# A four-layer diffusion backbone on one core: two activation tiles moved by 32 bytes in memory

## The chip, the cores and the metric

The kernel runs on one core of a Trainium2 chip. The metric is the time of one execution on the device in microseconds; the median of a few executions is compared. Profiles come from one profiled execution each.

## The reference

One inference step of a backbone with four layers, on 128 context tokens and 512 latent tokens of width 1024. Each layer is a token mixer and a squared-ReLU MLP, each with modulation, a gate, a scaled residual and a layer norm behind it:

```python
for l in range(DEPTH):                      # DEPTH = 4
    kind, j = l % N_MIXERS, l // N_MIXERS   # 0 linear attention, 1 conformer, 2 short convolution
    mp, ms = adaln(c_ctx, ...), adaln(c, ...)
    op, os_ = mixer(modulate(xp, mp[0], mp[1])), mixer(modulate(xs, ms[0], ms[1]))
    xp = layer_norm(ALPHA * xp + mp[2] * op, ln_g[l, 0], ln_b[l, 0])
    xs = layer_norm(ALPHA * xs + ms[2] * os_, ln_g[l, 0], ln_b[l, 0])
    fp = sqrelu_mlp(modulate(xp, mp[3], mp[4]), ff_w1[l], ff_w2[l])
    fs = sqrelu_mlp(modulate(xs, ms[3], ms[4]), ff_w1[l], ff_w2[l])
    xp = layer_norm(ALPHA * xp + mp[5] * fp, ln_g[l, 1], ln_b[l, 1])
    xs = layer_norm(ALPHA * xs + ms[5] * fs, ln_g[l, 1], ln_b[l, 1])

def sqrelu_mlp(h, w1, w2):                  # 1024 -> 4096 -> 1024
    return jnp.square(jax.nn.relu(h @ w1)) @ w2

def short_conv(h, w_in, w_conv, w_out, grid):
    bg, cg, u = jnp.split(h @ w_in, 3, axis=-1)
    u = dw_conv(cg * u, w_conv, GRID_W if grid else 1)
    return (bg * u) @ w_out
```

Layers 0 and 3 have linear attention, layer 1 the conformer convolution, layer 2 the short convolution.

## The kernel before

All 640 tokens (five token tiles of 128; tile 0 is the context) stay on the chip: x0 to x4 hold them token by token, and hT holds the next sublayer's input feature by feature, in eight k tiles of 128 features. Weights stream from memory in tiles of 128x1024 float32. To keep float32 accuracy with the faster number type float32r, every operand of a large product is split in two parts, hi and lo, and a product is three: hi·hi, hi·lo and lo·hi. For weights `split` (L104 to L109) does that: ScalarE copies hi into tile whi, VectorE subtracts and gives wlo. For activations the same is done in `put_hT` (L394 to L399) into hT, in the MLP's `evac` (L1156 to L1164) into tile act, and in the short convolution's `evac` (L1100 to L1125) into the tiles a0 to a7, called a in the profile.

There are two kinds of products, and TensorE's order is written by hand:

- mm1 (L138 to L172, product at L143): the weight tile is stationary, hT moves past it in a piece of 384 tokens and one of 256. One output bank takes 8 k tiles x 3 = 24 products.
- mm2 (L175 to L195, product at L189): the activations are stationary, 512 columns of a weight tile move past them. Again 24 products fill an output bank, one bank for each token tile; five banks are a pass over one half of the output's 1024 columns. The stationary operand is act in the MLP, a in the short convolution and hT in linear attention and the conformer. Banks are called mm and mx in the profile, by the pool that they come from.

```python
for h, a in ((0, 0), (0, 1), (1, 0)):
    self.nc.tensor.matmul(
        ps, lhs(kt, h, t), s[a][:, c + cols.start:c + cols.stop], start=(i == 0), stop=(i == 3 * nk - 1)
    )
```

The MLP (L1144 to L1180) goes over four blocks of 1024 hidden features. In each, mm1 makes eight act tiles, and mm2 runs two passes of 120 products with them. So a layer's MLP has eight passes, and in the very last one of the kernel the last token tile is done in two halves of 256 columns (`finish`, L900). The short convolution (L1086 to L1133) runs two passes with a, in `out_proj`.

Between these products stand others: transposes for the layer norm (L408), which `ln` puts 6.2 us behind a tile's statistics by a clock of the program's own, which counts a product of n columns as n / 2400 us (`beat`, L93); and, in the MLPs before layers 1 to 3, the modulation of the next layer. VectorE adds up that modulation's products in tile acc (L316 to L320), and TensorE sums acc over its partitions (L338) and transposes the result (L298).

Tiles of a sublayer come from a pool that is opened for it and gets the memory behind the permanent pools, in the order in which the tiles are declared. In the program before the change the tiles begin at these bytes of each partition: hT at 17696; the weight tiles at 104480 and every 4096 from there to 149536; acc at 178176; the two buffers of r at 182272 and 184832; the eight buffers of act at 187392 and every 5120 from there; in the short convolution cu0 at 178176, cu1 at 181280, a0 to a7 at 184384 and every 5120 from there, y at 225344. Divided by 64, hT and the weight tiles leave a rest of 32; acc, r, act, cu0, a and y leave 0. hT's parts for a k tile and a token tile lie at multiples of 512 bytes from its beginning, and so do those of act and a.

The conformer's pool begins at the same place, with u0 (4096 bytes) and u1 (4096 bytes), which GpSimd fills with zeros in this order.

Of the kernel before, what the change touches and what calls it, by code (L numbers as in the profile page):

```python
# [7 lines left out]
F32 = mybir.dt.float32  # L8
# [30 lines left out]
class Filler:  # L39
    """Products for the tensor engine to run while a chain of dependent steps waits for other engines."""  # L40

# [25 lines left out]
class Net:  # L67
# [19 lines left out]

# [1 line left out]
    def after(self, us, fn):  # L89
# [12 lines left out]

# [1 line left out]
    def split(self, src, n=1024):  # L104
# [14 lines left out]
    @contextmanager  # L119
    def behind(self, t):  # L120
        """Keeps the vector engine's work in it behind the parts of token tile t's next input."""
        with ExitStack() as held:
            for half in range(2 if (t, 0) in self.marks else 0):
                held.enter_context(self.tc.issue_after(self.marks[t, half]))
            yield
# [10 lines left out]

# [1 line left out]
    def mm1_steps(self, ps, w, c0, n, m=128):  # L138
        """Yields the microseconds of each instruction, as the other generators of products do."""
        i = 0  # L140
        for kt in range(KT):
            for a, h in ((0, 0), (0, 1), (1, 0)):
                self.nc.tensor.matmul(  # L143
                    ps[:m, :n], w[a][:, kt * m:(kt + 1) * m], self.hT[:, h, kt, c0:c0 + n],
                    start=(i == 0), stop=(i == 3 * KT - 1),
                )
                i += 1
                yield self.beat(n / 2400)
# [24 lines left out]

# [1 line left out]
    def mm2(self, srcs, lhs, epi):  # L175
# [31 lines left out]

# [1 line left out]
    def mod_queue(self, l):  # L209
        """Queues layer l's modulation by groups of 2048 columns: a k tile at a time on the tensor engine, or,  # L210
        where the groups fall in an MLP, two k tiles of 512 columns at a time on the vector engine."""
        self.mods[l] = {"T": self.modp.tile([128, 48, 2], F32, tag="modT", name="modT", bufs=3)}
        for g in range(1 if l == self.layers[0] else 0, 3):
            if (l, g) in MOD_DVE:
                for v in (2 * g, 2 * g + 1):
                    for half in range(2):
                        for p in range(4):
                            self.fill.append((l, g, partial(self.mod_dve, l, v, half, p)))
            else:
                for kt in range(KT):  # L220
                    self.fill.append((l, g, partial(self.mod_step, l, g, kt)))
# [21 lines left out]
    def tail(self, us, fn):  # L243
        """Runs fn once: us later, or before the next part of a modulation."""
        def once():
            if self.mod_tail is once:
                self.mod_tail = None
                fn()

        self.mod_tail = once  # L250
        self.after(us, once)

    def mod_bank(self, l, cols):
        """A bank for the sums, and the bias of each quarter of its rows."""
        ps = self.ps.tile([128, 512], F32, tag="md", name="md", bufs=1)
        mrow = self.row.tile([128, 512], F32, tag="mrow", name="mrow")
        n = 128 // len(cols)
        for t, c in enumerate(cols):
            self.nc.gpsimd.dma_start(
                mrow[n * t:n * t + n, :], self.d["mod_b"][l:l + 1, c:c + 512].broadcast_to([n, 512]))  # L260
        return ps, mrow
# [39 lines left out]
    def mod_dve(self, l, v, half, p):  # L301
        """Vector v's half: two k tiles more of the products, added up per partition; the tensor engine sums those."""
        nc, m = self.nc, self.mods[l]
# [44 lines left out]
    def affine(self, l, sub, prev):  # L348
        """A, B with modulate(LN(x)) = xhat * A + B per feature; prev = (l, i) of the LN."""
        nc = self.nc  # L350
# [23 lines left out]

# [1 line left out]
    def stats(self, a, b, eps):  # L376
        """mean, (var + eps) ** -0.5 and -mean * that over two [128, 512] halves."""
        nc = self.nc
        st = self.small.tile([128, 2, 6], F32, tag="bn", name="bn")
        nc.vector.bn_stats(st[:, 0], a)  # L380
        nc.vector.bn_stats(st[:, 1], b)
        mv = self.moments(st, eps)
        nc.gpsimd.tensor_scalar(out=mv[:, 4:5], in0=mv[:, 0:1], scalar1=mv[:, 3:4], scalar2=-1.0, op0=AL.mult, op1=AL.mult)
        return mv
# [9 lines left out]
    def put_hT(self, hf, k0, t):  # L394
        """hf [128, n, 128]: features of k tiles k0.. of token tile t, split into hT."""
        dst = lambda h: self.hT[:, h, k0:k0 + hf.shape[1], t * 128:(t + 1) * 128]
# [50 lines left out]

# [1 line left out]
    def start(self):  # L449
# [27 lines left out]
    def opening(self, products, raw, tmp):  # L477
        """The first sublayer's input, k tile by k tile as its shift and scale come in: unit u of the first
        layer's modulation holds those of features 128 u.. for all inputs. products(u): what tile u is for."""
        nc = self.nc  # L480
        parts = {}
# [56 lines left out]

# [1 line left out]
    def gla(self, l, j, nxt):  # L540
        nc, d, tc = self.nc, self.d, self.tc
        with ExitStack() as ctx:
# [8 lines left out]
            def gate_w(dst, hd):  # L551
                """Two heads of the gates' second factor, against z_hi, z_lo, z_hi and 1, 1: w_hi, w_hi, w_lo, b_hi, b_lo."""
                st = self.stage.tile([128, 1024], F32, tag="st", name="st")
# [112 lines left out]
            def chunks(a, par):  # L666
                """[128, 640] -> the chunks of one parity: [128, 5, 64]."""
                return a.rearrange("p (c b k) -> p c b k", b=2, k=64)[:, :, par]
# [4 lines left out]
            def core1(hd):  # L673
# [34 lines left out]
                for i in range(2):  # L708
# [3 lines left out]
                    self.mark = nc.vector.tensor_tensor(out=Em[i], in0=q[hd, 1], in1=Em[i], op=AL.mult)  # L712
                # per tile: the keys of the chunk that comes first, decayed to its end, and both chunks' decay
                F1 = q[hd, 0].rearrange("p (d c k) -> p d c k", d=2, k=64)
# [171 lines left out]
    def out_proj(self, w, lhs, nxt, last):  # L886
        """The sublayer's last product with the residual, and the layer norm token tile by token tile."""
        self.mm2(w[0], lhs, self.residual(0))
        self.out_last(w, lhs, nxt, last)
# [10 lines left out]
    def finish(self, w, lhs):  # L900
        """The last token tile, its second half of columns in two parts to have less to do after the last product."""
        nc, t = self.nc, TT - 1
# [31 lines left out]

# [1 line left out]
    def conformer(self, l, j, nxt):  # L936
        nc, d, tc = self.nc, self.d, self.tc
        with ExitStack() as ctx:
# [50 lines left out]
            def convolve(c, scr, meanwhile=None):  # L989
                """Four taps of 32 channels a pass: partition (s, channel) holds the row shifted by s."""  # L990
                f = 5 * ROW
# [21 lines left out]
            def add_bias():  # L1013
                """x += b_pw2 * gate, for the second product's bias."""
                self.flush()
# [68 lines left out]

# [1 line left out]
    def shortconv(self, l, j, nxt):  # L1086
        nc, d, tc = self.nc, self.d, self.tc
        with ExitStack() as ctx:
            sb = ctx.enter_context(tc.tile_pool(name="sc", bufs=1))
            cus = []  # L1090
            for i in range(2):
                cu = sb.tile([128, 770], F32, name=f"cu{i}")
                nc.gpsimd.memset(cu, 0.0)
                cus.append(cu)
# [47 lines left out]

# [1 line left out]
    def mlp(self, l, ln_next, last):  # L1144
        nc, d, tc = self.nc, self.d, self.tc
        with ExitStack() as ctx:
            sb = ctx.enter_context(tc.tile_pool(name="mlp", bufs=1))
            self.acc = sb.tile([128, 2, 512], F32, name="acc")
            self.load_gate(l, "g2")
# [37 lines left out]
    def more_banks(self, more):  # L1187
        """Three banks more for products, except where linear attention has them."""
        if not more:
# [23 lines left out]
def _layout(inp):  # L1213
# [3 lines left out]
    A = {}  # L1217
# [22 lines left out]
    def stat(w, order=None):  # L1240
        """[1024, M] -> output tiles [M/128, 128, 8 * 128]."""
        t = w.reshape(KT, 128, -1, 128).transpose(2, 1, 0, 3)
        return (t if order is None else t[order]).reshape(-1, 128, KT * 128)

    def mov(w):
        """[1024, 512 n] -> [n, 4, 128, 2 * 512]."""
        return w.reshape(4, 2, 128, -1, 512).transpose(3, 0, 2, 1, 4).reshape(-1, 4, 128, 1024)
# [51 lines left out]
```

## Time and profile before

| | |
|---|---|
| median of 3 runs | 3054.25 us |
| lowest and highest | 3054.06 and 3059.77 us |
| profiled execution, first to last instruction (span) | 3051.8 us |
| TensorE (PE) busy | 3003.6 us, 98%, 17452 products |
| its weight loads (PEld) | 2619.4 us, 86% |
| VectorE (DVE) busy | 1850.7 us, 61% |
| ScalarE (ACT) busy | 998.5 us, 33% |
| GpSimd (POOL) busy | 153.6 us, 5% |
| memory traffic, mean | 115 GB/s |
| mean granted clock of TensorE | 0.996 of full speed |

How to read it: "busy" is the time in which an engine had at least one instruction under way. Products overlap, so a product's own duration (its start to its end) is longer than the interval from its start to the next one's. A line such as L189 is the line of the kernel that issued the instruction; `mx<-whi,act` names the tile written and the tiles read. The profile does not say which of the tiles read is stationary; the code does.

### The profile page before, as it was taken

The numbers are of one execution on the slowest core, as the hardware profiler recorded it, in microseconds if no ns is written. First come the engines' busy times: TensorE is split into PE (matmuls) and PEld (weight loads), VectorE is DVE, ScalarE is ACT, GpSimd is POOL, SyncE is SP. The second block draws the span as 40 slices with busy tenths as digits, with TensorE's granted clock in tenths as the row PEclk, the third lists the DMA queues.
The fourth block names the chain that finished last, engine by engine and source line by source line (L and its number), as shares of the span: only waits on it lengthen the run. The fifth ranks groups of instructions, "written<-read, shape, count | busy, mean of one in ns | idle before, by whom it ended". The sixth has DMA issues, their size and how long they took to land.

```text
span 3051.8 us, 42170 instructions
## 1 busy us (share of the span) xinstructions
PE 3003.6 (98%) x17452; PEld 2619.4 (86%) x17452; DVE 1850.7 (61%) x2737; ACT 998.5 (33%) x1592; POOL 153.6 (5%) x295
## 2 busy tenths in 40 slices
PE   7999999999999899999999999999999999999998
PEld 5887798898898697888999988988988887998997
DVE  4445877767597775775384485773465448644345
ACT  4333433232242351332242152321344434322221
POOL 0000100000010010000010010000010001000000
PEclk9999999999999999999999999999999999999999
DMA  6334244445164425453232133552213312222120
GB/s 245 120 121 162 87 132 155 152 144 171 62 182 127 129 97 163 148 174 97 72 111 77 63 118 107 170 162 66 82 69 120 104 64 89 101 90 74 58 90 35
DMA packets 101792, 350.28 MB, mean 115 GB/s; under 512 B 12940, under 2 KB 18572, under 8 KB 101600
## 3 DMA queue, kind: packets, MB, share of 16 engines
q1 hardware_dynamic: 91888, 317.79, 31.6%
q0 software_dynamic: 9712, 29.80, 3.0%
q8 instruction: 137, 2.24, 0.3%
q14 instruction: 55, 0.45, 0.0%
HBM read 340.29 MB, written 7.24 MB: 114 GB/s over the span
## 4 chain that ended last, share of the span: by engine, by line
PE 95%; DVE 2%; DMA 1%; ACT 1%; issue 1%; POOL 0%; SPq 0%; DVEq 0%; POOLq 0%; ACTq 0%
PE mx L143 23%; PE mm L189 22%; PE mx L189 21%; PE mm L143 18%; PE md L273 1%; PE mx L1003 1%; PE md L338 1%; PE tp L408 1%; PE tp L777 1%; PE o L797 1%; PE o L763 1%; PE tp L747 1%; PE tp L724 1%; PE mm L1003 0%; ACT whi L107 0%
## 5 line engine op out<-in xcount | busy, mean ns | idle before, releaser
L107 ACT CAST whi<-st 128x1024 fp32r<-128x1024 f32 (+1 forms) x378 | 395.7, 1050 | 1118.1 <-PE mx L189 301.4
L143 PE MATMUL mx<-hT,whi 128*128 128x256 f32 (+1 forms) x3216 | 706.8, 310 | 1.6 <-DVE hT L398 1.3
L108 DVE TENSOR_TENSOR wlo<-st,whi 128x1024 fp32r<-128x1024 f32 (+1 forms) x378 | 460.0, 1221 | 377.7 <-ACT whi L107 375.9
L143 PE MATMUL mm<-hT,whi 128*128 128x384 f32 (+1 forms) x2592 | 566.6, 309 | 1.2 <-DVE hT L398 0.7
L143 PEld LDWEIGHTS mx<-hT,whi 128*128 128x128 f32 x3216 | 541.9, 189 | 6.0 <-DVE hT L398 2.8
L143 PE MATMUL mx<-hT,wlo 128*128 128x384 f32 (+1 forms) x1608 | 497.8, 310 | 0.0
L189 PE MATMUL mx<-whi,act 128*128 128x512 f32 (+1 forms) x1536 | 493.6, 395 | 0.0
L143 PEld LDWEIGHTS mm<-hT,whi 128*128 128x128 f32 x2592 | 434.1, 189 | 5.4 <-DVE hT L398 1.6
L143 PE MATMUL mm<-hT,wlo 128*128 128x256 f32 (+1 forms) x1296 | 399.7, 308 | 0.0
L189 PEld LDWEIGHTS mx<-whi,act 128*128 128x128 f32 x1536 | 287.4, 187 | 70.8 <-issue 1.7
L189 PE MATMUL mm<-whi,act 128*128 128x512 f32 (+1 forms) x1040 | 336.2, 394 | 0.0
L143 PEld LDWEIGHTS mx<-hT,wlo 128*128 128x128 f32 x1608 | 304.4, 189 | 2.5 <-issue 2.5
L189 PE MATMUL mx<-wlo,act 128*128 128x512 f32 (+1 forms) x768 | 303.4, 395 | 0.0
L320 DVE SCALAR_TENSOR_TENSOR acc<-st,cm,acc 128x512 f32<-128x512 f32 x392 | 275.8, 745 | 36.0 <-ACT acc L318 34.6
L189 PE MATMUL mm<-whi,hT 128*128 128x512 f32 x888 | 286.1, 395 | 0.0
L143 PEld LDWEIGHTS mm<-hT,wlo 128*128 128x128 f32 x1296 | 245.3, 189 | 7.2 <-issue 6.7
L189 PEld LDWEIGHTS mm<-whi,act 128*128 128x128 f32 x1040 | 194.5, 187 | 47.8 <-issue 1.7
L189 PE MATMUL mm<-wlo,act 128*128 128x512 f32 (+1 forms) x520 | 205.1, 394 | 0.0
L189 PEld LDWEIGHTS mm<-whi,hT 128*128 128x128 f32 x888 | 165.5, 188 | 31.9
L204 DVE TENSOR_TENSOR mx<-mx,gate 128x512 f32<-128x512 f32 x120 | 83.5, 696 | 172.7 <-PE mx L189 172.6
L189 PEld LDWEIGHTS mx<-wlo,act 128*128 128x128 f32 x768 | 144.0, 187 | 41.0 <-issue 7.5
L189 PE MATMUL mm<-wlo,hT 128*128 128x512 f32 x444 | 177.3, 399 | 0.0
(250 smaller groups left out, 3157.8 us busy)
## 6 DMA issues: line engine op xcount, KB each, us to landing
st<-in_w SPq DMA_DIRECT2D x256, 512.0 KB, 3.6
st<-in_modv SPq DMA_DIRECT2D x112, 512.0 KB, 4.1
st<-in_modw SPq DMA_DIRECT2D x80, 512.0 KB, 4.7
st<-in_gvr SPq DMA_DIRECT2D x32, 512.0 KB, 5.5
st<-in_cpw SPq DMA_DIRECT2D x24, 512.0 KB, 4.9
st<-in_scin SPq DMA_DIRECT2D x24, 512.0 KB, 3.5
ur<-uscr SPq DMA_DIRECT2D x40, 238.0 KB, 5.9
st<-in_gqk SPq DMA_DIRECT2D x16, 512.0 KB, 5.1
```

The lines of the kernel that those rows point to most:

```text
L107: self.nc.scalar.copy(hi[:, :n], src)
L108: self.nc.vector.tensor_tensor(out=lo[:, :n], in0=src, in1=hi[:, :n].bitcast(F32), op=AL.subtract)
L143: self.nc.tensor.matmul(ps[:m, :n], w[a][:, kt * m:(kt + 1) * m], self.hT[:, h, kt, c0:c0 + n], start=(i == 0), stop=(i == 3 * KT - 1),)
L189: self.nc.tensor.matmul(ps, lhs(kt, h, t), s[a][:, c + cols.start:c + cols.stop], start=(i == 0), stop=(i == 3 * nk - 1))
L204: self.nc.vector.tensor_tensor(out=ps, in0=ps, in1=g, op=AL.mult)
L273: nc.tensor.matmul(ps[32 * t:32 * t + 32, :], self.cm[:, kt, :], st[t // 2][:, c:c + 512], start=(kt == 0), stop=(kt == KT - 1),)
L320: nc.vector.scalar_tensor_tensor(out=acc[:, s], in0=w, scalar=c, in1=acc[:, s], op0=AL.mult, op1=AL.add)
L338: nc.tensor.matmul(ps[r:r + 32, :], self.ones, acc[:, s], start=True, stop=True)
L408: nc.tensor.transpose(tp[:, i * 128:(i + 1) * 128], x[:, k * 128:(k + 1) * 128], self.ident)
L724: nc.tensor.matmul(sp[:, i, dd], self.tri[:, 2 + dd], G[:, t0 + i, dd], start=True, stop=True)
L747: nc.tensor.matmul(sc[:, i], Em[i][:, ts], Ep[i][:, ts], start=True, stop=True)
L763: nc.tensor.matmul(o[t], P[t % 2][:, 2], v[t], start=(t % 2 == 0), stop=False)
```

## The change

Tile acc of the MLP gets 8 more columns of float32 (32 bytes) and is used through a view of the old shape. Everything declared behind it in that pool, r and act, begins 32 bytes later. In the short convolution cu0 gets 8 more columns, so cu1, a and y begin 32 bytes later: act at 187424, a0 at 184416. The work is otherwise the same. The rest of the diff takes out comments and docstrings and changes no instruction.

```diff
 # shortconv
             for i in range(2):
-                cu = sb.tile([128, 770], F32, name=f"cu{i}")
+                cu = sb.tile([128, 770 + 8 * (1 - i)], F32, name=f"cu{i}")
                 nc.gpsimd.memset(cu, 0.0)
                 cus.append(cu)
 # mlp
             sb = ctx.enter_context(tc.tile_pool(name="mlp", bufs=1))
-            self.acc = sb.tile([128, 2, 512], F32, name="acc")
+            self.acc = sb.tile([128, 1032], F32, name="acc")[:, :1024].rearrange("p (s c) -> p s c", s=2)
```

## Rows read from the trace of the kernel before

**Rows 1.** The page: span, TensorE's busy time, the chain that ended last by engine.

```profile
span 3051.8 us, 42170 instructions
...
PE 3003.6 (98%) x17452; PEld 2619.4 (86%) x17452; DVE 1850.7 (61%) x2737; ACT 998.5 (33%) x1592; POOL 153.6 (5%) x295
...
PE 95%; DVE 2%; DMA 1%; ACT 1%; issue 1%; POOL 0%; SPq 0%; DVEq 0%; POOLq 0%; ACTq 0%
```

**Rows 2.** TensorE's waits: who waited for whom, us in total, times, longest.

```profile
PE mx L189 <- DVE x L205: 2.5, 2, 1.3
...
PE mx L143 <- DVE hT L398: 1.3, 4, 0.5
```

**Rows 3.** Groups of L189, TensorE: shape, count | busy us, mean ns | idle before.

```profile
L189 PE MATMUL mx<-whi,act 128*128 128x512 f32 x1520 | 490.8, 396 | 0.0
...
L189 PE MATMUL mm<-whi,act 128*128 128x512 f32 x1024 | 333.3, 395 | 0.0
...
L189 PE MATMUL mx<-wlo,act 128*128 128x512 f32 x760 | 301.2, 396 | 0.0
L189 PE MATMUL mm<-whi,hT 128*128 128x512 f32 x888 | 286.1, 395 | 0.0
...
L189 PE MATMUL mm<-wlo,act 128*128 128x512 f32 x512 | 202.9, 396 | 0.0
```

**Rows 4.** Timeline of TensorE, first products of banks: start us, us, what.

```profile
597.34 0.39 PE L189 MATMUL mm<-whi,act 128*128 128x512 f32 x1
...
608.54 0.39 PE L189 MATMUL mm<-whi,act 128*128 128x512 f32 x1
...
1055.76 0.39 PE L189 MATMUL mx<-whi,hT 128*128 128x512 f32 x1
...
1066.64 0.39 PE L189 MATMUL mx<-whi,hT 128*128 128x512 f32 x1
...
1738.65 0.40 PE L189 MATMUL mm<-whi,a 128*128 128x512 f32 x1
...
1749.85 0.40 PE L189 MATMUL mm<-whi,a 128*128 128x512 f32 x1
```

**Rows 5.** Windows: us, busy PE, PEld, DVE, ACT, POOL (count), clock, DMA share, GB/s.

```profile
585.00:614.00 29.00, 29.00 (x125) 22.43 (x124) 22.19 (x31) 4.49 (x5) 3.01 (x6) 1.00 0.55 174
...
1733.00:1762.00 29.00, 29.00 (x127) 23.36 (x127) 14.18 (x18) 5.54 (x6) 0.00 (x0) 1.00 0.10 35
```

**Rows 6.** Timeline of TensorE behind eight transposes in the conformer, every third product.

```profile
1074.55 0.39 PE L189 MATMUL mx<-wlo,hT 128*128 128x512 f32 x1
...
1075.24 0.39 PE L189 MATMUL mx<-wlo,hT 128*128 128x512 f32 x1
...
1075.94 0.39 PE L189 MATMUL mx<-wlo,hT 128*128 128x512 f32 x1
...
1076.62 0.39 PE L189 MATMUL mx<-wlo,hT 128*128 128x512 f32 x1
```

**Rows 7.** Timeline in shortconv: a tile's normalisation on ScalarE, its transposes on TensorE.

```profile
1777.27 0.82 ACT L426 ACTIVATE x<-x,mv 128x512 f32<-128x512 f32 x1 [0.30 <-POOL mv L383]
...
1780.12 1.04 PE L408 MATMUL tp<-ident,x 128*128 128x128 f32 x8
```

**Rows 8.** Timeline of TensorE, products of 256 columns: mm1, then the last token tile.

```profile
628.19 0.28 PE L143 MATMUL mx<-hT,wlo 128*128 128x256 f32 x1
...
629.27 0.28 PE L143 MATMUL mx<-hT,wlo 128*128 128x256 f32 x1
...
3036.30 0.28 PE L189 MATMUL mx<-wlo,act 128*128 128x256 f32 x1
...
3038.78 0.28 PE L189 MATMUL mx<-wlo,act 128*128 128x256 f32 x1
```

**Rows 9.** Groups of VectorE: writes of 640 columns to act and to hT.

```profile
L1163 DVE TENSOR_TENSOR act<-r,act 128x640 fp32r<-128x640 f32 x128 | 105.4, 823 | 67.3 <-ACT act L1162 67.2
...
L531 DVE TENSOR_TENSOR hT<-h,hT 128x640 fp32r<-128x640 f32 x8 | 6.5, 818 | 0.9 <-ACT hT L530 0.8
```

## The prediction

> **What bounds the kernel now.** I read the page's busy shares first: TensorE is busy in 98% of the 3051.8 us span, and the chain that ended last lies on it for 95% [rows 1]. So the time is the number of products times the interval from one start to the next. Next the list of TensorE's waits: the only entry on a product of L189, where act and a are used, is 2.5 us behind x [rows 2], and the list of groups shows that the 128x512 products of act had no idle time before them [rows 3]. A faster feed would cure nothing there; the interval is what is left to look at.
>
> The mean duration of a product does not show it. 128x512 products take 395 or 396 ns with act stationary and 395 ns with hT [rows 3], because they overlap. The timeline does show it. One output bank takes 24 products, and the bank's name changes between mm and mx, so the first products of banks can be subtracted. With act stationary, two banks go from 597.34 to 608.54: 11.20 us for 48 products, **233.3 ns** each. With a stationary, 1738.65 to 1749.85: again 11.20 us, **233.3 ns**. With hT stationary, 1055.76 to 1066.64: 10.88 us, **226.7 ns** [rows 4]. The moving operand is of one kind in all three (a 512-column half of a weight tile), as are width, number type and count. The stationary tile differs.
>
> Is it traffic on the chip? The table of windows says no [rows 5]. Both stretches have a granted clock of 1.00 (the 2.4 GHz level); around act VectorE is busy for 22.2 of 29 us at a DMA share of 0.55, around a for 14.2 of 29 us at 0.10, and the interval is the same. What act and a share, and hT does not, is their place by 64 bytes: rest 0, against 32 for hT and for the weight tiles that stream past them.
>
> **The change part by part.**
>
> *Products of act and a.* With act there are 1520 + 1024 + 760 + 512 = 3816 products of 512 columns [rows 3], with a 2 passes of 5 token tiles of 24, which is 240: together 4056. After the change both tiles have the rest of hT. If that sets the interval, each product starts 6.67 ns sooner: 4056 x 6.67 ns = **27.0 us** off TensorE, which is the path.
>
> [...]
>
> *Finding the short interval again after a break.* Behind eight transposes (L408) three products of hT take 0.69 us (1074.55 to 1075.24), the next three 0.70 us (to 1075.94), and then 0.68 again (to 1076.62) [rows 6]. That is 0.03 us lost per break, which act at its present interval need not lose. The lower count of breaks is the 17 starts behind mm1 (16 blocks of the four MLPs and the short convolution; the second pass of each follows the first directly), 17 x 0.03 = 0.5 us. The upper count adds every group of transposes of the layer norms (7 sublayers x 5 tiles x 2 = 70) and every group of modulation sums (14 vectors x 2 halves = 28): 115 x 0.03 = 3.5 us. Many of those fall between products of mm1 or of hT, so I take half, 58 breaks: **1.7 us** given back.
>
> *Layer norm behind the last product.* The code puts a tile's transposes 6.2 us of its own clock behind its statistics, and that clock counts 213 ns a product. TensorE now gets there 0.2 us sooner (6.2 / 0.213 = 29 products x 6.67 ns). In shortconv the transposes of a tile start at 1780.12, and the normalisation that they read ends at 1777.27 + 0.82 = 1778.09 [rows 7]: 2 us of slack hide 0.2. The first products of the next mm1 do wait for the split of hT, 1.3 us in four waits [rows 2], and that chain starts at the last products. The lower end is 0. The upper end gives back all that is saved in the last pass of the four sublayers that use act or a and are followed by another: 4 x 120 x 6.67 ns = 3.2 us. The existing waits are short, nearest to the lower end: **0.3 us** given back.
>
> *The last token tile.* Its second half of columns runs as 48 products of 256 columns. With act these take 118.1 ns (3036.30 to 3038.78, 2.48 us for 21). Products of this width in mm1, both of whose operands have rest 32, take 120.0 ns (628.19 to 629.27, 1.08 us for 9) [rows 8]. So equal rests are 1.9 ns slower at this width: 48 x 1.9 ns = 0.1 us, left out of the sum.
>
> *The other engines on the moved tiles.* r, act, cu1, a and y move along. VectorE subtracts 128x640 in 823 ns to act (rest 0) and in 818 ns to hT (rest 32) [rows 9]: nothing to see beyond 5 ns, and ScalarE's copies, of which I show no row, are bounded alike. act and a are written 136 times, each by a copy and a subtraction, all beside products; were that cover gone, 136 x 2 x 5 ns = 1.4 us either way. The memset of cu0 has 8 more elements on GpSimd. All of this costs nothing on the path.
>
> *Waits between pools.* A shift by 32 bytes could make a tile overlap one more old tile. By the sizes the one new overlap is at the conformer's start, u1 with the end of acc, and u0 already waits for acc, ahead of it on the same queue. No DMA moves past another. Nothing is added.
>
> *Sum:* -27.0 + 1.7 + 0.3 = -25.0 us. The profiled span of 3051.8 us becomes 3026.8. The median of the runs, 3054.25 us, is 2.45 us above the span, which is what lies around it, and becomes **3029.3 us**.
>
> **The rivals.**
>
> *No effect, since the interval goes by something else (0.11).* act and a lie in the upper part of the memory and hT in the lower, and their steps between k tiles differ (5120 and 2560 bytes). A rule by region or by step would explain the three intervals as well, and the change touches neither: 3054 us. The same time would come if the shift were rounded away, but the addresses are multiples of 32, so 32 bytes do move a tile. Against it: in mm1 the weights, from a third region, are stationary, and 120.0 ns [rows 8] exceeds 256 columns at 2.4 GHz (106.7) by 13.3 ns, just as hT's 226.7 exceeds 213.3. Only act and a exceed it by 20.0. [...]
>
> *Slower, since equal rests settle at a worse interval (0.04).* At 256 columns this is seen: 120.0 against 118.1 ns. If act at 512 columns did the same, which decides itself at 233.3 ns, the price would be 4056 x 1.9 ns = 7.7 us: 3062 us. Against it stands hT at 512 columns.
>
> *Half the gain, since breaks come too often (0.05).* If act stayed in the unsettled 0.69 to 0.70 us for three [rows 6] in half of its products, about 13.5 us would be gained: 3040.7 us. Against it: hT settles within six to eight products, and a bank has 24.
>
> **How the numbers follow.** The forecast has 0.80. Its own bounds are gains of 27.0 - 0.5 + 1.4 = 27.9 and 27.0 - 3.5 - 3.2 - 1.4 = 18.9 us, 3026.4 to 3035.4. The runs shown spread to 5.5 us above the median, so I reach to 3042, which also takes in the half gain, and to 3024 below. No effect and slower stay outside. A measurement of this kernel can tell about 0.2% (6.1 us) from no change; within that lies the second case alone: faster 0.85, same 0.11, slower 0.04.
>
> **What would show it.** Right: two banks of act or a in 10.88 us in place of 11.20; the counts of products and the intervals of hT and mm1 as before; the span near 3027; TensorE's list of waits longer by under 1 us. Wrong: act still at 233.3 ns (no effect); a at 233.3 with act at 226.7 (a coarser rest than that by 64 counts, since a then differs from hT by 128); act above 233.3 (slower); or short intervals and a span that does not follow (a wait behind the last products has taken the gain).

## The result and the profile after

Four runs of the changed kernel have a median of **3030.83 us** (3028.88 to 3034.11). Four runs of the kernel before, beside them, have 3056.91 us (3054.06 to 3059.77). The ratio is 0.9916, with a 95% interval of 0.9902 to 0.993, so the change takes off 26.1 us, within 21 and 30. The forecast was 3029.3 us and a gain of 25.0. The sum came true; one of its parts, a's, did not.

The page of the kernel after, beside [rows 1]: span and count, busy time, the chain that ended last by engine.

```profile
span 3032.4 us, 42170 instructions
...
PE 2983.9 (98%) x17452; PEld 2623.9 (87%) x17452; DVE 1850.3 (61%) x2737; ACT 999.6 (33%) x1592; POOL 153.8 (5%) x295
...
PE 95%; DMA 2%; DVE 1%; ACT 1%; issue 1%; POOL 0%; SPq 0%; DVEq 0%; ACTq 0%; POOLq 0%
```

TensorE is busy for 19.7 us less, which is all of the 19.4 us by which the profiled span is shorter. Nothing else moved: counts are equal, VectorE and ScalarE differ by about 1 us, and the chain still lies on TensorE. On every engine the instructions stand in the order of before.

TensorE's waits, beside [rows 2]: who waited for whom, us in total, times, longest.

```profile
PE mx L189 <- DVE x L205: 2.5, 2, 1.3
...
PE mx L143 <- DVE hT L398: 1.4, 4, 0.6
...
PE mm L143 <- DVE hT L398: 0.8, 2, 0.6
PE mm L143 <- DVE wlo L108: 0.6, 1, 0.6
```

The wait on L189 is what it was, the waits for hT grew by 0.1 us each (the second was 0.7 us before), a third one for hT, of 0.2 us, and one of 0.6 us for a weight tile's lo part are new in the list. Elsewhere the wait of the products o for S in linear attention (L797) grew from 0.3 to 1.1 us, and that for weights at the start (L487) shrank from 11.7 to 10.8. The whole list adds up to 38.4 us, where it was 38.0: TensorE still has hardly anything to wait for.

The groups of L189 with act, beside [rows 3]: shape, count | busy us, mean ns | idle before.

```profile
L189 PE MATMUL mx<-whi,act 128*128 128x512 f32 x1520 | 481.8, 390 | 0.0
...
L189 PE MATMUL mm<-whi,act 128*128 128x512 f32 x1024 | 327.1, 390 | 0.0
...
L189 PE MATMUL mx<-wlo,act 128*128 128x512 f32 x760 | 296.9, 391 | 0.0
...
L189 PE MATMUL mm<-wlo,act 128*128 128x512 f32 x512 | 200.0, 391 | 0.0
```

Busy time of the first group falls by 9.0 us and that of the second by 6.2; the mean duration falls by 5 or 6 ns. But hT had a mean of 395 ns all along [rows 3], with the short interval, so the mean duration still does not rank the tiles. The starts do.

TensorE's timeline in the kernel after (start us, us, what), beside [rows 4, 6, 8]: a break in act, the first products of act's banks, then those of hT and of a, and the 256 columns of the last token tile.

```profile
592.42 1.05 PE L338 MATMUL md<-acc,ones 128*32 128x512 f32 x4
...
594.20 0.40 PE L189 MATMUL mx<-wlo,act 128*128 128x512 f32 x1
...
594.89 0.39 PE L189 MATMUL mm<-wlo,act 128*128 128x512 f32 x1
...
595.58 0.39 PE L189 MATMUL mm<-wlo,act 128*128 128x512 f32 x1
...
596.26 0.39 PE L189 MATMUL mm<-wlo,act 128*128 128x512 f32 x1
...
600.11 0.39 PE L189 MATMUL mx<-whi,act 128*128 128x512 f32 x1
...
605.55 0.39 PE L189 MATMUL mm<-whi,act 128*128 128x512 f32 x1
...
1053.02 0.39 PE L189 MATMUL mx<-whi,hT 128*128 128x512 f32 x1
...
1063.90 0.39 PE L189 MATMUL mx<-whi,hT 128*128 128x512 f32 x1
...
1730.47 0.39 PE L189 MATMUL mm<-whi,a 128*128 128x512 f32 x1
...
1741.67 0.39 PE L189 MATMUL mm<-whi,a 128*128 128x512 f32 x1
...
3017.56 0.28 PE L189 MATMUL mx<-wlo,act 128*128 128x256 f32 x1
...
3019.36 0.28 PE L189 MATMUL mx<-wlo,act 128*128 128x256 f32 x1
```

From 600.11 to 605.55 a bank of 24 products with act takes 5.44 us, **226.7 ns** each where it was 233.3. hT is as before: 10.88 us for two banks. **a is as before too**: 11.20 us for two banks, 233.3 ns, though it was moved by the same 32 bytes. That is what the experiments are about.

### The profile page after: what moved, and what is told of

Read it like the earlier page. It is cut to its first block, busy times and chain, and to the rows that moved or that the text cites. A ratio compares the mean times of both kernels' runs of the same rounds, so it can differ in the third digit from the quotient of the medians.

```text
span 3032.4 us, 42170 instructions
## 1 busy us (share of the span) xinstructions
PE 2983.9 (98%) x17452; PEld 2623.9 (87%) x17452; DVE 1850.3 (61%) x2737; ACT 999.6 (33%) x1592; POOL 153.8 (5%) x295
## 4 chain that ended last, share of the span: by engine, by line
PE 95%; DMA 2%; DVE 1%; ACT 1%; issue 1%; POOL 0%; SPq 0%; DVEq 0%; ACTq 0%; POOLq 0%
PE mx L143 23%; PE mm L189 22%; PE mx L189 20%; PE mm L143 19%; PE md L273 1%; PE md L338 1%; PE mx L1003 1%; PE tp L408 1%; PE o L797 1%; PE tp L777 1%; PE tp L724 1%; PE o L763 1%; DMA st<-in_gvr 1%; PE tp L747 1%; PE mm L1003 1%
## 5 line engine op out<-in xcount | busy, mean ns | idle before, releaser
L189 PE MATMUL mx<-whi,act 128*128 128x512 f32 (+1 forms) x1536 | 484.7, 389 | 0.0
L189 PEld LDWEIGHTS mx<-whi,act 128*128 128x128 f32 x1536 | 287.9, 188 | 61.2 <-issue 1.7
L189 PE MATMUL mm<-whi,act 128*128 128x512 f32 (+1 forms) x1040 | 330.2, 388 | 0.0
L189 PE MATMUL mx<-wlo,act 128*128 128x512 f32 (+1 forms) x768 | 299.2, 390 | 0.0
L189 PE MATMUL mm<-whi,hT 128*128 128x512 f32 x888 | 286.1, 395 | 0.0
L189 PEld LDWEIGHTS mm<-whi,act 128*128 128x128 f32 x1040 | 194.8, 188 | 41.3 <-issue 1.7
L189 PE MATMUL mm<-wlo,act 128*128 128x512 f32 (+1 forms) x520 | 202.3, 389 | 0.0
L189 PEld LDWEIGHTS mm<-whi,hT 128*128 128x128 f32 x888 | 165.5, 188 | 31.9
L189 PE MATMUL mm<-wlo,hT 128*128 128x512 f32 x444 | 177.3, 399 | 0.0
L189 PEld LDWEIGHTS mx<-wlo,act 128*128 128x128 f32 x768 | 144.2, 188 | 36.2 <-issue 7.5
```

The costliest lines, as they stand in the source:

```text
L189: self.nc.tensor.matmul(ps, lhs(kt, h, t), s[a][:, c + cols.start:c + cols.stop], start=(i == 0), stop=(i == 3 * nk - 1))
```

## Experiments

The reading on record was that a stationary tile is quick when it has the moving tile's rest by 64 bytes. a refutes it. The weight tiles and hT lie at 32 by 256; act went from 0 to 32; a went from 64 to 96. Four readings were left: the two operands need equal rests by 128; by 256; the stationary tile alone needs a certain rest, wherever the weights are; or the region of a tile, or the sublayer that uses it, decides. Moving a alone tells the first two apart; moving the weights alone tells them from the last two. All diffs below are against the kernel after. Line numbers shift by one or two where lines were added.

**a 64 bytes further** (a at 160 by 256: the weights' rest by 128 and not by 256).

```diff
-                cu = sb.tile([128, 770 + 8 * (1 - i)], F32, name=f"cu{i}")
+                cu = sb.tile([128, 770 + 24 * (1 - i)], F32, name=f"cu{i}")
```

> cu0 gets 24 columns more instead of 8, so that a begins another 64 bytes later (184480) and has the rest of hT and the weights by 128 (32) and not only by 64. Theory 1 (equal rest by 128 of the stationary and the moving tile): two banks of a go from 11.20 to 10.88 us, 240 x 6.67 ns = 1.6 us in all. Theory 2 (equal rest by 64 is enough, and a is slow for another reason of its stage): a stays at 11.20 us. Theory 3 (the stationary tile has to have rest 32 by 128, wherever the moving one begins): 10.88 us, like theory 1. act stays at 226.7 ns by all three. The whole time differs from the changed kernel by 1.6 us at most, too little to be seen.

Measured: 3031.23 us (3027.37 to 3032.47), ratio to before 0.9921, interval 0.9899 to 0.9943. Its timeline, two banks with a:

```profile
1730.01 0.39 PE L189 MATMUL mm<-whi,a 128*128 128x512 f32 x1
...
1741.17 0.39 PE L189 MATMUL mm<-whi,a 128*128 128x512 f32 x1
```

11.16 us for 48 products, 232.5 ns. The rest by 128 is not enough, and a certain rest of the stationary tile by 128 is not either. What this run leaves is theory 2, and the rest by 256, at which a now differs from the weights by 128.

**Many rests in one kernel, twice.** Tiles act and a get 128 bytes more and are used through a view that starts some elements in, another number in each layer. The small tile "sums" has three buffers in place of four, which moves what follows 32 bytes down, and acc and cu0 have their old widths again; the shifts allow for both (the lines for a, sums, acc and cu0 are not shown). The rests by 128 are 16, 64, 48, 8 in layers 0 to 3 and 80 for a in the first kernel, and 96, 112, 4, 36 and 32 in the second (SHIFT 0, 4, 9, 17, SHIFT_A 0).

```diff
+SHIFT, SHIFT_A = (12, 24, 20, 10), 12
...
-                    a = sb.tile([128, 2, NTOK], F32R, tag="act", name="act", bufs=8)
+                    a = sb.tile([128, 2 * NTOK + 32], F32R, tag="act", name="act", bufs=8)
+                    a = a[:, SHIFT[l]:SHIFT[l] + 2 * NTOK].rearrange("p (h n) -> p h n", h=2)
```

> act's rest by 128 is set layer by layer: 16, 64, 48 and 8 in the MLPs of layers 0 to 3, and a has 80; the weights keep 32. (The tiles get 128 bytes more each and are used through shifted views.) Theory 1: 233.3 ns in all five, none at 226.7, and the time is that of the kernel before the change within 3 us. Theory 2: the same except that nothing changes for rests that are not equal by 64. A graded rule (the nearer the rests, the shorter) gives intervals between 226.7 and 233.3 ns at 16 and 48. If there is a rest that is better than equal ones, one of these may be below 226.7 ns.

> As the kernel with rests 16, 64, 48, 8 and 80, with 96, 112, 4 and 36 for act in layers 0 to 3 and 32 for a. Theory 1: a at 226.7 ns, act at 233.3 ns in all four layers. Theory 2: act at 226.7 ns in layer 0 (96 and 32 are equal by 64) and at 233.3 ns in the others. A rule by 16-byte lines has rest 36 (layer 3) with 32 and rest 4 with 0. If 36 is short as well, a difference of 4 bytes does not matter.

Measured: 3052.04 us and 3050.10 us, one run each, near the 3054.43 us of the kernel before on that chip. Two banks of layer 1 (rest 64) in the first kernel's timeline:

```profile
1526.25 0.40 PE L190 MATMUL mm<-whi,act 128*128 128x512 f32 x1
...
1537.45 0.40 PE L190 MATMUL mm<-whi,act 128*128 128x512 f32 x1
```

and of a (rest 32 by 128) in the second's:

```profile
1738.33 0.39 PE L190 MATMUL mm<-whi,a 128*128 128x512 f32 x1
...
1749.47 0.40 PE L190 MATMUL mm<-whi,a 128*128 128x512 f32 x1
```

11.20 us and 11.14 us, 233.3 and 232.1 ns; the other layers lie between 11.12 and 11.20. So a missed what theory 1 said of it, and act in layer 0 of the second kernel what theory 2 said. The 128 extra bytes blur the question by 256, since from one buffer to the next they move that rest by 128. So in the second kernel every other buffer of a had exactly the weights' rest by 256, and three products in a row at equal rests were not enough to bring the interval down (232.1 ns). What holds is that no rest tried is quicker than 226.7, nor settles there but for one bank of layer 2 in each kernel.

**The weights moved instead.** A tile of 96 bytes ahead of the pool of the incoming weights moves the weight tiles and everything behind them. By 256 the weights now have 128, act 128, a 0; hT is not moved and keeps 32.

```diff
+        self.gap = pool("gap")
+        self.gap.tile([128, 24], F32, name="gap")
         self.stage = pool("stage", 5)
...
-                cu = sb.tile([128, 770 + 8 * (1 - i)], F32, name=f"cu{i}")
+                cu = sb.tile([128, 770 + 24 * (1 - i)], F32, name=f"cu{i}")
```

> 96 bytes are put in front of the staging tiles, so that everything behind them moves: weights, act and a all have rest 0 by 128, hT keeps 32. Theory 1 (rests relative to each other): act and a at 226.7 ns; hT as the stationary tile goes to 233.3 ns (about 1680 products, 11 us); in mm1 weights and hT are no longer equal, the 384-column products go from 173.3 to 180.0 ns (4352 x 6.67 = 29 us) and the 256-column ones from 120.0 to about 118 (8 us less), so about 3060 us. Theory 3 (the stationary tile at rest 32): act and a back at 233.3 ns, hT as stationary stays at 226.7 ns, mm1 slower as above, about 3075 us. Theory 4 (it goes by regions of the memory): nothing changes against the kernel after the change.

Measured: 3035.74 us in one run. Its timeline, two banks each of hT, act and a:

```profile
1049.38 0.39 PE L191 MATMUL mm<-whi,hT 128*128 128x512 f32 x1
...
1060.58 0.39 PE L191 MATMUL mm<-whi,hT 128*128 128x512 f32 x1
...
1520.18 0.39 PE L191 MATMUL mm<-whi,act 128*128 128x512 f32 x1
...
1531.06 0.39 PE L191 MATMUL mm<-whi,act 128*128 128x512 f32 x1
...
1732.08 0.40 PE L191 MATMUL mm<-whi,a 128*128 128x512 f32 x1
...
1743.28 0.40 PE L191 MATMUL mm<-whi,a 128*128 128x512 f32 x1
```

This decides it. hT stayed where it was and went from 10.88 to **11.20 us**; act moved along with the weights and stayed at 10.88. So it is the place of the two operands to each other that counts, and neither a region nor a rest of the stationary tile alone. a stayed at 11.20: it has the weights' rest by 128 here (0), which theory 1 took for enough, but by 256 it is at 0 and they are at 128. The two places are not independent in effect: products whose stationary tile nobody moved start every 233.3 ns in place of 226.7.

One more expectation missed: mm1, whose operands now differ too, did not slow. The mean interval at 384 columns over all its products, worked out from the starts in the timeline, is 173.6 ns against 173.7. That is the main reason why the whole time is 3035.74 us and not the 3060 expected.

**a at the weights' rest by 256** (32).

```diff
-                cu = sb.tile([128, 770 + 8 * (1 - i)], F32, name=f"cu{i}")
+                cu = sb.tile([128, 770 + 56 * (1 - i)], F32, name=f"cu{i}")
```

> cu0 gets 56 columns more in place of 8, so that a begins at 184608: rest 32 by 256, as hT, act and the weights have it (by 256 a left 96 in the changed kernel and 160 where it was moved by another 64 bytes). Theory 1b (the interval is short when the stationary and the moving tile have the same rest by 256): two banks of a take 10.88 us, 1.6 us less in all than in the changed kernel. Theory 2 (a is slow for another reason of its stage): a stays near 11.2 us. The whole time is within 2 us of the changed kernel either way.

Measured: **3027.44 us** (3025.88 to 3027.57), ratio to before 0.9907, interval 0.9891 to 0.9924. Two banks with a in its timeline:

```profile
1727.19 0.39 PE L189 MATMUL mm<-whi,a 128*128 128x512 f32 x1
...
1738.07 0.39 PE L189 MATMUL mm<-whi,a 128*128 128x512 f32 x1
```

10.88 us: a is quick at last, in the same stage, so theory 2 is out. Nothing coarser than 256 is needed: divided by 512, a leaves 288 here and hT leaves 288, the weights 32, and both tiles are quick. This is the version to keep; for a alone the gain is 240 x 6.67 ns = 1.6 us, too little for the runs to tell from the kernel after (the intervals overlap), and seen in the timeline only.

**Four other rests by 256**, with the buffers' steps untouched: acc is widened by layer, and act lies at 160, 224, 96 and 64 in layers 0 to 3, a at 0.

```diff
-            self.acc = sb.tile([128, 1032], F32, name="acc")[:, :1024].rearrange("p (s c) -> p s c", s=2)
+            self.acc = sb.tile([128, 1024 + (40, 56, 24, 16)[l]], F32, name="acc")[:, :1024].rearrange("p (s c) -> p s c", s=2)
...
-                cu = sb.tile([128, 770 + 8 * (1 - i)], F32, name=f"cu{i}")
+                cu = sb.tile([128, 770 + 48 * (1 - i)], F32, name=f"cu{i}")
```

> acc is widened layer by layer by 160, 224, 96 and 64 bytes in place of 32, so act's rest by 256 is 160, 224, 96 and 64 in the MLPs of layers 0 to 3, against 32 of the weights; a has 0. Theory 1b (by 256): all of them at 232 to 233.4 ns, whole time near the kernel before the change. Theory 1 (by 128, and a slow for another reason): layer 0 (160 and 32 are equal by 128) at 226.7 ns, the other three near 233.3 ns, which would give back 6.5 us of the 27. A tile is not slow for what else it is: if one of these layers is short and not layer 0, both fall.

Measured: 3051.39 us in one run. Its timeline, two banks each of layers 0 and 1:

```profile
678.73 0.39 PE L189 MATMUL mm<-whi,act 128*128 128x512 f32 x1
...
689.92 0.39 PE L189 MATMUL mm<-whi,act 128*128 128x512 f32 x1
...
1524.21 0.39 PE L189 MATMUL mm<-whi,act 128*128 128x512 f32 x1
...
1535.20 0.39 PE L189 MATMUL mm<-whi,act 128*128 128x512 f32 x1
```

Layer 0 (128 bytes off) takes 11.19 us, 233.1 ns, in these two banks and 11.15 in most others; layers 2 and 3 take 11.20. Equal rests by 128 are not enough, now with clean steps. Layer 1 (192 bytes ahead, or 64 behind) takes 10.99 us, 229.0 ns: a value in between, which none of the readings gave.

**Is it the role or the width?** mm1 did not mind unequal rests at 384 columns. Here its pieces are 512 and 128 columns, once with equal rests and once with the shift of the weights above (second diff, and cu0 as there, on top of the first). In both kernels the first four feature tiles of a sublayer read the previous sublayer's hT for the last 128 tokens of the 512-column piece; the work done is otherwise the same.

```diff
-CA, CB = 384, 256
+CA, CB = 512, 128
```

```diff
+        self.gap = pool("gap")
+        self.gap.tile([128, 24], F32, name="gap")
         self.stage = pool("stage", 5)
```

> The changed kernel with its pieces of tokens in mm1 and the like at 512 and 128 columns in place of 384 and 256. If the width decides (the interval depends on the rests at 512 columns and hardly at 384), mm1's 512-column products, whose two operands have the same rest, take 226.7 ns, as in mm2. If it is the role (which of the two tiles is stationary), nothing is said about this number beforehand: 226.7 or 233.3. [...] Slower as a whole by 8720 / 2 x (226.7 + 115 - 173.3 - 120) ns = 210 us.

> The same pieces of 512 and 128 columns with the weights, act and a moved as in the kernel that puts 96 bytes in front of the staging tiles: weights have another rest than hT. If the width decides, mm1's 512-column products go from 226.7 to 233.3 ns, although it is the moving tile that has the other rest now and the stationary one that is the weights. If the role decides, they stay where they are with equal rests.

Measured: 3255.59 us and 3288.02 us, one run each. mm1 in the timeline with equal rests:

```profile
432.64 0.39 PE L143 MATMUL mx<-hT,wlo 128*128 128x512 f32 x1
...
435.36 0.39 PE L143 MATMUL mx<-hT,wlo 128*128 128x512 f32 x1
```

and with unequal ones:

```profile
439.18 0.40 PE L145 MATMUL mx<-hT,wlo 128*128 128x512 f32 x1
...
444.10 0.40 PE L145 MATMUL mx<-hT,wlo 128*128 128x512 f32 x1
```

2.72 us for 12 products, 226.7 ns, and 4.92 us for 21, 234.3 ns. So it is the width: at 512 columns products with the weights as stationary tile lose about as much as act's did (7.6 ns in these rows and 5.8 by the means of all such products, 6.7 there). (Both kernels are slow as a whole because of the products of 128 columns: in the timeline with equal rests 24 of them take 2.63 us, 435.58 to 438.21, 110 ns each. That is 0.86 ns a column, where 512 columns take 0.44. The 115 ns in the expectation's sum was the author's estimate, which no run shows.)

**How fine is it?** hT is used through a view 4 bytes, then 16 bytes into a tile of 256 bytes more, so that nothing else changes its rest. act and a have the weights' rest.

```diff
-        self.hT = const.tile([128, 2, KT, NTOK], F32R, name="hT")
+        self.hT = const.tile([128, 2 * KT * NTOK + 64], F32R, name="hT")[:, 1:1 + 2 * KT * NTOK].rearrange("p (h k n) -> p h k n", h=2, k=KT)
...
-                cu = sb.tile([128, 770 + 8 * (1 - i)], F32, name=f"cu{i}")
+                cu = sb.tile([128, 770 + 56 * (1 - i)], F32, name=f"cu{i}")
```

> hT is used through a view 4 bytes into a wider tile, and nothing else moves by 256: hT leaves 36, the weights, act and a leave 32. If equality has to be exact, hT as the stationary tile of mm2 (conformer, linear attention) goes from 226.7 ns at rest to 232 or more; act and a stay at 226.7. If it is decided by lines of 16 bytes or more, hT stays at 226.7 (36 and 32 begin in one line of 16). mm1 at 384 and 256 columns within 1 ns as before. Whole time up to 9 us above the kernel with a by 256, or the same.

> The same with 16 bytes: hT leaves 48. If a difference of a 16-byte line matters, hT as stationary is at 232 ns or more; if only some part of 256 bytes above that does (as 32 bytes did in the kernel before the change), it stays at 226.7.

Measured: 3058.70 us and 3034.74 us, one run each (before on the same chip: 3055.83). With 4 bytes, the timeline has mm1 at 256 columns and then two banks with hT stationary:

```profile
643.50 0.28 PE L143 MATMUL mm<-hT,wlo 128*128 128x256 f32 x1
...
645.35 0.29 PE L143 MATMUL mm<-hT,wlo 128*128 128x256 f32 x1
...
1057.33 0.39 PE L189 MATMUL mm<-whi,hT 128*128 128x512 f32 x1
...
1068.47 0.40 PE L189 MATMUL mm<-whi,hT 128*128 128x512 f32 x1
```

Two banks take 11.14 us, 232.1 ns: one float is enough to lose the short interval. mm1, which was expected within 1 ns, takes 1.85 us for 15 products of 256 columns, 123.3 ns against 120.0. By the means over all pairs of starts, against the version with a at 32, that is 1680 products of hT x 4.3 ns + 4368 x 3.1 (256 columns) + 4368 x 2.0 (384) = 29.5 us, of the 31.3 us by which the span is longer (3056.9 against 3025.6). The sublayers' input, off by one float, costs more than the whole change brought.

With 16 bytes the timeline holds something else: two banks of the conformer, then one in layer 3.

```profile
1047.17 0.39 PE L189 MATMUL mm<-whi,hT 128*128 128x512 f32 x1
...
1058.37 0.39 PE L189 MATMUL mm<-whi,hT 128*128 128x512 f32 x1
...
2559.59 1.03 PE L408 MATMUL tp<-ident,x 128*128 128x128 f32 x8
...
2561.39 0.39 PE L189 MATMUL mx<-wlo,hT 128*128 128x512 f32 x1
...
2565.47 0.39 PE L189 MATMUL mx<-wlo,hT 128*128 128x512 f32 x1
```

The first takes 11.20 us for 48, 233.3 ns. But behind the transposes at 2559.59 the same pair of tiles runs 18 products in 4.08 us, 226.7 ns. Of the 44 banks of hT whose last ten products follow each other without a break, 14 ran short in this way. So unequal rests do not forbid the short interval; they let TensorE settle in a long one, and which of the two follows a break is not fixed. With 4 bytes between them, 96 (hT with the weights moved) or 128 (act in layer 0 of the four rests) no bank ran short. mm1 changed here as well: by the means 384 columns lose 1.6 ns and 256 columns gain 1.2.

## Why the prediction was right, and where it was not

**The interval as bound: right.** TensorE's 98%, the waits and the mean duration all left only the interval, and the time followed it. The full clock that the prediction puts at 2.4 GHz is in its rows as a rate: hT's 226.7 ns less the 120.0 of mm1 is 106.7 ns for 256 columns more, 2.4 columns a nanosecond, and the granted clock was 1.00 in both windows of [rows 5]. The intervals between the starts of act's products, summed over the same 3766 pairs in both traces, fall from 882.0 to 858.4 us, by 23.6 us. The sums for a (55.3 us) and for hT (369.8 us) did not change.

**The products of act and a: act right, a wrong.** act's 3816 products were to bring 25.4 us at the settled 6.67 ns, and act settled there. a's 240 were to bring 1.6 us and brought nothing. The step that failed is "both tiles have the rest of hT": a rest by 64 bytes. The rest that counts is by 256, at which act was moved onto the weights (0 to 32) and a past them (64 to 96). The prediction named that outcome, a left at 233.3 with act at 226.7, as the mark of a coarser rule; it had not asked which rules the rows allowed. hT and the weights are equal by 256 as well, so the rows could not tell 64 from 256, and the addresses of a under each rule were there to be worked out. The median came out 1.5 us above the forecast, about what a was to bring; but the runs spread more than that, and against the runs of before taken beside it the gain was 26.1 us, 1.1 more than forecast. So neither median tells whether a won, and that the sum came within about 1 us with one part missing is luck; the timeline alone shows the part.

**Breaks: right.** 3766 pairs at 6.67 ns would be 25.1 us and 23.6 came, so 1.5 us went to finding the interval again. 1.7 had been said; that was a choice between 0.5 and 3.5, and that it lay so near is partly luck. Behind the sums at 592.42 act takes 0.69 us for three products, from 594.20 to 594.89 and again to 595.58, then 0.68 to 596.26: the pattern of [rows 6].

**Layer norm and pools: right.** The two waits for hT in the list grew by 0.2 us together and the third adds 0.2, where 0.3 was allowed; L408 is not in the list of waits, and no new wait stands at the start of a pool. The 0.6 us for wlo was not in the sum: a quicker TensorE reaches one weight tile before VectorE has split it.

**256 columns: right.** From 3017.56 to 3019.36 are 15 products, 120.0 ns, where unequal rests had 118.1. **The other engines: right.** VectorE's writes to act still take 823 ns, and the kernel with a at 32 changes neither VectorE's nor ScalarE's busy time by over 1 us (1850.0 and 998.2 us).

**The profiled execution** ran 5.6 us over the span forecast for it (3026.8). A window over the conformer shows why: us, then busy PE, PEld, DVE, ACT, POOL with counts, the granted clock, DMA share, GB/s. In the kernel after:

```profile
969.00:1044.00 75.00, 67.07 (x532) 47.52 (x531) 54.76 (x77) 23.83 (x55) 7.01 (x16) 0.91 0.37 112
```

The same stretch in the kernel before, 6 us later on its clock:

```profile
975.00:1050.00 75.00, 67.30 (x546) 47.86 (x546) 55.14 (x77) 27.11 (x64) 7.00 (x16) 0.95 0.36 112
```

And in the version with a at 32:

```profile
969.00:1044.00 75.00, 66.67 (x553) 49.05 (x552) 55.65 (x77) 26.90 (x63) 6.99 (x16) 0.98 0.38 116
```

The stretch is the one where TensorE has gaps, 8 of 75 us, and in part of it the granted clock was 0.50: in the kernel after from 997 to 1003 us, from 1011 to 1013.9 and from 1024.5 to 1027.5, in the kernel before from 1004 to 1007 and from 1014.2 to 1017. How much differs from run to run: as an estimate from the means of 0.91, 0.95 and 0.98, 9% of 75 us, 6.8 us of work, were lost in this one, 3.8 in the run of before and 1.5 with a at 32. With that the sums nearly close: from the span with a at 32 to the span after are 6.8 us, next to 5.3 of clock and the 1.5 that the intervals of a won there (55.3 to 53.8 us). And against before, 19.4 us of span and 3.0 us of clock make 22.4 us, next to the 23.6 us that act won less some tenths of waits. These are shares of two digits, and what each of the three runs has at a clock of 0.50 outside the window is taken as equal (in the runs after and before that is part of the start, the end and one short stretch, at 2379 us after and 2393 before). No row ties the clock to the change: runs of the kernel before have a mean of 0.994 to 0.997 for the whole, those of the kernel after 0.995 or 0.996.

**The rivals.** "No effect" fell with act (233.3 to 226.7 ns), and the experiment with the weights moved excludes its region and step, since hT, which stayed, went from 226.7 to 233.3. "Slower" fell: 512 columns do not go as 256 do, which went from 118.1 to 120.0. "Half the gain" fell: behind the sums at 592.42 act settles within seven products, and from 595.13 on its starts lie 226.7 ns apart.

## What to carry to other kernels

When TensorE never waits, read the starts of its products, not their durations, and compare one width with different stationary tiles: a constant difference can come from where tiles lie, as the 6.67 ns did here. For float32r products like these, print the addresses of all large operands and give stationary and moving tiles of 512-column products the same rest by 256 bytes, with steps between buffers that are multiples of 256 (5120 is one; with 5248 a took 232.1 ns). When a rule is read off a few examples, list each rule that fits them and work out every moved tile's place under each; here that would have set a right without a run.

## What the runs showed that was not expected

- In these float32r products the interval hangs on the places of both operands to each other, exact to one float: equal rests by 256 give 226.7 ns at 512 columns; operands 4, 16, 32, 64, 96 or 128 bytes apart give 232 to 234 (16 not always, see below), and act 64 bytes behind the weights 229.0.
- It hangs on width. Between equal and unequal rests 512 columns lose 5 to 8 ns (2 in the case of 229.0), 384 columns between nothing (96 bytes apart) and 2 ns (4 bytes), and 256 columns gain 1 or 2 ns, but lose 3 when hT is 4 bytes off (123.3 for 120.0). No run moves the weights by 4 bytes, so whether the distance does that or hT's own place is open.
- With 16 bytes between the tiles, the long interval is one of two that TensorE can settle in after a break: 14 of 44 banks found the short one.
- With equal rests, products of 512 and of 256 columns take 226.7 and 120.0 ns: 106.7 for 256 columns more, 2.4 columns a nanosecond, and 13.3 ns beside the columns.

What inside the chip joins the two operands is open: no run here shows it, nor what chooses between the two intervals (233.3 and 226.7 ns) that one pair of tiles had 16 bytes apart.
